# A hybrid decoder layer on one core: gate and up projections as seven products of half blocks

## The chip, the cores and the metric

The kernel runs on 1 core of one Trainium2 chip. The metric is the device time in microseconds (us) of one execution; lower is better. The five engines have queues of their own and run side by side: TensorE (PE in the profile), VectorE (DVE), ScalarE (ACT), GpSimd (POOL) and SyncE (SP), which issues nearly all DMAs here.

## The reference, cut to what matters

512 tokens of width 1024 in float32 pass through one layer: a norm and an input projection, two token mixers (a recurrence and a three-branch attention), an output projection with residual, and a SwiGLU feed-forward of width 2816. The change is in the last:

```python
D_MODEL = 1024; SEQ = 512; D_FF = 2816
h = rms_norm(x, ffn_norm_w[l])
x = x + (jax.nn.silu(h @ w_gate[l]) * (h @ w_up[l])) @ w_down[l]
```

## The kernel before, in words

All matrix operands are split into two float32r parts, `hi` (a rounded copy, made by ScalarE) and `lo` (the difference, made by a subtraction on VectorE or GpSimd), and a product of two such operands is three matmuls (`mm3`, L98). A weight tile of 512 KB comes through `load` (L111, SP's queue) into a `raw` tile, of which there are three, and `weights` (L130) makes its two parts: the cast on ScalarE (L146), the subtraction on VectorE or, in the input projection, GpSimd (L147). Activations of the feed-forward lie transposed in `ar`, as 8 chunks of 128 channels by two halves of 256 tokens, each in both parts.

The program's time falls in three stages. Up to about 180 us come the input projection and the recurrence, up to about 315 us the attention, a block of 128 tokens at a time (tiles 3, 2, 1, 0) with `out_proj` (L858) and `norm2` (L867) of a finished tile in between; `norm2` writes the second norm's transposes into `ar` (the subtraction is L885). Then SwiGLU: 11 groups of 256 hidden columns. `load_group` (L932) loads four raw tiles (gate and up, two halves of the channels); `gate_up` (L940) forms for each 128 columns the gate sums `fg` and the up sums `fu` over 8 chunks, 24 matmuls each, then the activation (L950 to L952) and the split of the result into `gh` and `gl` (L953, L107). The first two groups run by halves of the tokens, 256 columns at a time, so that tokens 256 to 511 go ahead while the attention of the others ends; the other nine take all 512. I call the gate and up work of 128 hidden columns a **unit**; there are 22.

```python
    for grp in range(SPLIT):
        load_group(grp)
        gate_up(grp, 256, 512, (4, 6), (5, 7))
    for grp in range(SPLIT):
        gate_up(grp, 0, 256, (4, 6), (5, 7))
    for grp in range(SPLIT, DF // 256):
        load_group(grp)
        gate_up(grp, 0, T, (4, 6, 0), (5, 7, 2))
```

The down projection (`fd`, L968 on) takes two halves of 512 output columns; each steps through the 22 blocks of `gh`, `gl` with four token tiles, and adds the residual from `x_sb` (L996). The order of instructions on each engine is set when the program is built, by a scheduler with a model of times; on the chip each engine takes its queue in that order.

Of the kernel before, what the change touches and what calls it, by code (L numbers as in the profile page):

```python
# [20 lines left out]
P = 128  # L21
T = 512
# [16 lines left out]
# rows of the packed parameter vectors  # L39
# [10 lines left out]
def hybrid_layer(ctx, tc, x, pos, pack, w_in, gate_a, gate_x, qnw, knw, ck1, ck2, cv1, cv2, w_out, fnw, w_gate, w_up, w_down, out):  # L50
# [5 lines left out]
    wst = ctx.enter_context(tc.tile_pool(name="wst", bufs=4))  # L56
# [11 lines left out]
    SLOTS = {"qk": 16, "yr": 8, "rt": 8, "y": 4, "tr": 6}  # L68
# [6 lines left out]
    def rot(s, banks):  # L75
        """the next of a set of banks that a kind of tile takes in turn"""
        rota[s] = rota.get(s, -1) + 1
        return bank(s, banks[rota[s] % len(banks)])

    def b2(s, dt=F32, tag="tr"):  # L80
        return big.tile([P, 512], dt, tag=tag, name=nm(s), bufs=SLOTS[tag])

# [12 lines left out]
    def mm(o, l, r, start, stop):  # L95
        PE.matmul(o, lhsT=l, rhs=r, start=start, stop=stop)  # L96

    def mm3(o, l, r, start, stop):  # L98
        mm(o, l[0], r[0], start, False)
        mm(o, l[0], r[1], False, False)  # L100
        mm(o, l[1], r[0], False, stop)
# [27 lines left out]

    def weights(src, a, b, lo_eng=None, row=None, halves=False):  # L130
        """rows of a weight matrix, scaled by the parameter column of each block of rows if there is one, as a pair of
        float32r parts whose sum is exact"""
        raw = wst.tile([P, 1024], F32, tag="raw", bufs=3, name=nm("raw"))
        rv = raw[:, : a * b].rearrange("p (a b) -> p a b", a=a)
        load(rv, src)
        hi = wst.tile([P, 1024], F32R, tag="whi", name=nm("whi"))
        lo = wst.tile([P, 1024], F32R, tag="wlo", name=nm("wlo"))
        n = a * b
        if row is not None:
# [8 lines left out]
        return [tuple(t[:, : a * b].rearrange("p (a b) -> p a b", a=a)[:, i] for t in (hi, lo)) for i in range(a)]  # L148

# [1 line left out]
    x_sb = per.tile([P, NT, D], F32, name="x_sb")  # L151
# [5 lines left out]
    def load_x(t):  # L157
        load(x_sb[:, t], x[t * P : (t + 1) * P])
# [83 lines left out]
    def proj_cm(c0, banks):  # L242
        """channel-major projection of 512 columns from c0: four banks [128 channels, 512 tokens]"""
# [27 lines left out]
    for t in range(NT):  # L271
        dg = b2("dg", tag="qk")[:, :P]
# [45 lines left out]
    # softplus(-lambda), accurately, for the four channel tiles  # L318
# [34 lines left out]
    # block-diagonal gate weights  # L353
    gwr = wst.tile([P, 8, P], F32, tag="raw", bufs=3, name="gwr")
# [5 lines left out]
    gwh = [b2("gwh", F32R, tag="qk") for _ in range(2)]  # L360
    gwl = [b2("gwl", F32R, tag="qk") for _ in range(2)]
# [14 lines left out]
    for m in range(4):  # L376
# [6 lines left out]
        h, l = b2("xch", F32R, tag="qk"), b2("xcl", F32R, tag="qk")  # L383
# [15 lines left out]
    def head_rstd(ss, nt):  # L399
        """ss [P, nt, heads]: sums of squares of raw projections -> factors that rms-normalise them, in place"""  # L400
# [14 lines left out]
    def rotate(raw, rs, t0, nt, rows=P):  # L415
        """raw [rows, heads, 64] times rs [rows, heads], then the rotation of nt groups of heads by table columns from t0"""
# [27 lines left out]
    # values of a block of keys, with a column of ones that yields the softmax's sums  # L444
# [6 lines left out]
    zs = []  # L451
    for m in range(4):
        z = b2("z", tag="qk")
# [17 lines left out]
    def recurrence_a():  # L471
        for m in range(4):
# [6 lines left out]
            # d = 1/(1+v): seed (1+a)/2 and one Newton step, kept negated  # L479
# [17 lines left out]
    def recurrence_b():  # L497
        for m in range(4):
            after(S.activation(vs_[m], vs_[m], AF.Sqrt), *tanhs)
        for m in range(4):  # L500
# [6 lines left out]
            h, l = b2("yrh", F32R, tag="yr"), b2("yrl", F32R, tag="yr")  # L507
# [43 lines left out]
    def key_part(src, t, br):  # L551
        """raw keys times the norm weight, and their sums of squares"""
# [6 lines left out]
    # rows that pick the negated maxima of a branch  # L559
# [6 lines left out]
    def keys(br, banks):  # L566
        """normalise, rotate, split, transpose -> [kh;kh] and [kl;sel]"""
        head_rstd(kss[br], NT)
        rotate(kraw[br].rearrange("p t h d -> p (t h) d"), kss[br].rearrange("p t h -> p (t h)"), 0, NT)
        for g in range(2):  # L570
# [5 lines left out]
            pair = []  # L576
            for z in (h, l):
# [19 lines left out]
    # compressed branch: operand tiles [(l mod 2, d), tokens]  # L597
# [41 lines left out]
    # second operand of the transposed scores: the queries' high parts, and rows for the negated maxima of each branch  # L639
# [12 lines left out]
    # compress MLPs  # L652
# [5 lines left out]
    for j in range(2):  # L658
# [5 lines left out]
        for kk in range(4):  # L664
            raw = wst.tile([P, 4, HID], F32, tag="raw", bufs=3, name=nm("raw"))
# [98 lines left out]
    def front(i, g, br):  # L764
        """row maxima of the scores of the four heads of a group, negated, into rows of the second operand: a list of steps"""
# [28 lines left out]
    def back(i, g, br):  # L794
        """transposed scores less the maxima, their exponentials and the products with the values: a list of steps"""
# [22 lines left out]
    def merge(i, g, br):  # L818
        """a branch's outputs, divided by the softmax's sums and gated"""
# [16 lines left out]
    def finish(i):  # L836
        """the norm's factor, and the outputs transposed and split"""
# [190 lines left out]
```

## Time and profile before

| | |
|---|---|
| time, median of 3 runs | 692.53 us (691.77 to 693.9) |
| profiled execution, span from first to last instruction | 691.3 us |
| time around the span, as median less span | 1.2 us |
| busy: PE, DVE, ACT, POOL | 657.2, 365.4, 240.6, 103.1 us |
| instructions in the span | 8803 |

The profile is of one execution of this kernel; the own time of that execution is not listed apart from the three runs, so its span and the median are set side by side. "Busy" is the time in which an engine had an instruction under way, waiting for a shared resource after it was issued included. Lines such as L96 or L107 are helpers that many steps share; which step a row belongs to is told by its tile names.

### The profile page before, as it was taken

What the parts mean: (1) busy time and instruction counts of PE and PEld (TensorE: products, weight loads), DVE (VectorE), ACT (ScalarE), POOL (GpSimd) and SP (SyncE); (2) the same over time, 40 slices, a digit from 0 to 9 for tenths busy, and PEclk for the clock granted to TensorE, in tenths of its full rate; (3) what the DMA queues carried; (4) which work ended last, traced back from release to release, by engine and by line L of the source; (5) the groups of instructions that cost most, each with busy time, mean ns of one, the idle gap of its engine ahead of it and who ended that gap; (6) DMA issues with size and microseconds to landing.
All of it is one profiled execution on the core that took longest, in us unless ns stands there. A gap on an engine that the chain in (4) does not pass through costs nothing.

```text
span 691.3 us, 8803 instructions
## 1 busy us (share of the span) xinstructions
PE 657.2 (95%) x3486; PEld 543.6 (79%) x3486; DVE 365.4 (53%) x713; ACT 240.6 (35%) x409; POOL 103.1 (15%) x95
## 2 busy tenths in 40 slices
PE   7998959598999999999999999999999999999998
PEld 6876848575777888879898888888888888888886
DVE  6779999956455758584723443334433442223211
ACT  5516753473433335353412232223322331112110
POOL 3426596223400101011000000000000000000000
PEclk9999989899999999999999999999999999999999
DMA  7343210324501201032402442244223423334301
GB/s 255 97 126 91 62 34 24 105 62 157 182 10 53 62 1 31 1 93 61 122 1 61 122 108 71 66 122 122 69 73 103 121 94 100 110 108 138 92 1 61
DMA packets 45185, 58.30 MB, mean 84 GB/s; under 512 B 3860, under 2 KB 31832, under 8 KB 45144
## 3 DMA queue, kind: packets, MB, share of 16 engines
q1 hardware_dynamic: 45064, 57.71, 27.6%
q8 instruction: 27, 0.44, 0.3%
q14 instruction: 14, 0.11, 0.0%
q10 hardware_dynamic: 80, 0.03, 0.0%
HBM read 55.64 MB, written 2.10 MB: 84 GB/s over the span
## 4 chain that ended last, share of the span: by engine, by line
PE 74%; DVE 15%; issue 4%; DMA 3%; ACT 2%; POOL 1%; SPq 0%; POOLq 0%; DVEq 0%; ACTq 0%
PE fd L96 18%; PE fu L96 17%; PE fg L96 17%; PE po L96 5%; PE por L96 3%; PE sT L96 3%; PE pw L96 2%; PE s L96 2%; PE ph L96 2%; PE ptm L96 2%; DMA raw<-in_w_in_dram 1%; DVE xc L382 1%; DVE tg L484 1%; DMA raw<-in_cv_dram 1%; DVE tg L503 1%
## 5 line engine op out<-in xcount | busy, mean ns | idle before, releaser
L146 ACT CAST whi<-raw 128x1024 fp32r<-128x1024 f32 (+2 forms) x85 | 86.7, 1024 | 157.6 <-PE fd L96 75.4
L147 DVE TENSOR_TENSOR wlo<-raw,whi 128x1024 fp32r<-128x1024 f32 (+1 forms) x63 | 76.1, 1208 | 115.9 <-ACT whi L146 115.9
L96 PE MATMUL fu<-ar,whi 128*128 128x512 f32 (+1 forms) x352 | 101.9, 374 | 0.0
L96 PE MATMUL fg<-ar,whi 128*128 128x512 f32 x288 | 90.5, 395 | 0.0
L96 PEld LDWEIGHTS fu<-ar,whi 128*128 128x128 f32 x352 | 63.8, 188 | 13.1
L96 PE MATMUL fd<-wlo,gh 128*128 128x512 f32 (+1 forms) x189 | 69.3, 367 | 0.0
L96 PE MATMUL fd<-whi,gh 128*128 128x512 f32 (+1 forms) x189 | 69.2, 366 | 0.0
L96 PE MATMUL fd<-whi,gl 128*128 128x512 f32 (+1 forms) x189 | 68.9, 366 | 0.0
L96 PE MATMUL fu<-ar,wlo 128*128 128x512 f32 (+1 forms) x176 | 65.8, 374 | 0.0
L96 PEld LDWEIGHTS fg<-ar,whi 128*128 128x128 f32 x288 | 54.1, 188 | 13.0
L96 PE MATMUL ptm<-whi,ar 128*128 128x512 f32 (+1 forms) x192 | 56.1, 374 | 7.7 <-DVE qraw L526 7.7
L147 POOL TENSOR_TENSOR wlo<-raw,whi 128x1024 fp32r<-128x1024 f32 (+1 forms) x22 | 51.0, 2327 | 46.0 <-ACT whi L146 25.3
L96 PE MATMUL fg<-ar,wlo 128*128 128x512 f32 x144 | 57.0, 396 | 0.0
L96 PEld LDWEIGHTS ptm<-whi,ar 128*128 128x128 f32 x192 | 36.3, 198 | 13.6 <-DVE qraw L526 8.1
L96 PE MATMUL pcm<-ar,whi 128*128 128x512 f32 (+1 forms) x160 | 42.1, 354 | 1.4 <-DVE ar L226 1.0
L952 DVE SCALAR_TENSOR_TENSOR ft<-ft,fu 128x512 f32<-128x512 f32 (+1 forms) x26 | 15.7, 606 | 48.9 <-PE fu L96 48.9
L96 PE MATMUL po<-va,pe 128*128 128x65 f32 x320 | 41.1, 272 | 0.0
L96 PEld LDWEIGHTS po<-va,pe 128*128 128x128 f32 x320 | 39.7, 192 | 1.7 <-ACT pe L809 0.8
L96 PEld LDWEIGHTS fd<-whi,gh 128*128 128x128 f32 x189 | 35.6, 189 | 6.1
L96 PEld LDWEIGHTS fd<-wlo,gh 128*128 128x128 f32 x189 | 35.6, 189 | 5.9
L96 PEld LDWEIGHTS fd<-whi,gl 128*128 128x128 f32 x189 | 35.6, 188 | 5.9
L96 PEld LDWEIGHTS fu<-ar,wlo 128*128 128x128 f32 x176 | 33.1, 188 | 6.6
(315 smaller groups left out, 1149.4 us busy)
## 6 DMA issues: line engine op xcount, KB each, us to landing
raw<-in_w_gate_dram SPq DMA_DIRECT2D x22, 512.0 KB, 3.8
raw<-in_w_up_dram SPq DMA_DIRECT2D x22, 512.0 KB, 3.8
raw<-in_w_down_dram SPq DMA_DIRECT2D x22, 512.0 KB, 3.8
raw<-in_w_in_dram SPq DMA_DIRECT2D x16, 512.0 KB, 4.5
raw<-in_w_out_dram SPq DMA_DIRECT2D x8, 512.0 KB, 4.3
x_sb<-in_x_dram SPq DMA_DIRECT2D x4, 512.0 KB, 8.6
raw<-in_ck_dram SPq DMA_DIRECT2D x4, 512.0 KB, 3.9
raw<-in_cv_dram SPq DMA_DIRECT2D x4, 512.0 KB, 4.2
```

Source lines behind the costliest of these rows:

```text
L96: PE.matmul(o, lhsT=l, rhs=r, start=start, stop=stop)
L146: S.copy(hi[:, c], raw[:, c])
L147: (lo_eng or V).tensor_tensor(out=lo[:, c], in0=raw[:, c], in1=f(hi[:, c]), op=ALU.subtract)
L382: V.scalar_tensor_tensor(out=c[:, s:], in0=xr[:, : T - s], scalar=col(R_CW + 4 * k + m), in1=c[:, s:], op0=ALU.mult, op1=ALU.add)
L484: V.scalar_tensor_tensor(out=e, in0=v, scalar=1.0, in1=u, op0=ALU.subtract, op1=ALU.mult)
L503: V.tensor_tensor_scan(out=bx, data0=a, data1=bx, initial=0.0, op0=ALU.mult, op1=ALU.add)
L952: V.scalar_tensor_tensor(out=tt, in0=tt, scalar=0.5, in1=pu[:, :nn], op0=ALU.mult, op1=ALU.mult)
```

## The change

The gate rows and the up rows of a unit are stacked, and channels and tokens are halved: A11, A12 are the gate weights of channels 0 to 511 and 512 to 1023, A21, A22 the up weights; B11, B21 are the two channel halves of tokens 256 to 511, B12, B22 those of tokens 0 to 255. The 2 by 2 block product, eight half products, is formed as seven, by Strassen's identity in Winograd's form: A11 B11, A12 B21, S1 T1, S2 T2, S3 T3, S4 B22 and A22 T4 (the sign of T4 turned), with sums of weight blocks S1 to S4 and of activations T1 to T4, and sums of products afterwards.

- Weights: a unit loads `r1` (gate) and `r2` (up), 128 columns each, 512 KB each, into `raw` tiles, of which there are still three. GpSimd forms the four sums (`sums`), and ScalarE and VectorE split `r1`, `sb` (S2, S4), `sa` (S1, S3) and half of `r2` (`split`). Their tiles come from one set of 12 (`w`) in place of two sets of 4.
- Products: 7 times 12 matmuls of 256 columns, in three accumulators. ScalarE copies five intermediate values out of PSUM, GpSimd adds three of them (L1091 to L1093), VectorE the last two (L1028, L1029), then the activation follows (L1032 to L1034).
- `norm2`: the last two tiles (tokens 0 to 255) form T1 to T4 and transpose five tiles each in place of two.
- The gate weights of the first three units are loaded twice, and their products A11 B11 and A12 B21 go ahead of the rest, in place of the two groups by halves.
- The gated values stay unsplit until the end of the stage; `gh` and `gl` are then made in space that the operands leave. The residual is stored to DRAM by `out_proj` and loaded back in the down projection, which adds four stores and four loads of 512 KB.

The core of the diff (helpers and renamings left out):

```diff
-    wst = ctx.enter_context(tc.tile_pool(name="wst", bufs=4))
+    wst = ctx.enter_context(tc.tile_pool(name="wst", bufs=12))
...
+    def raw_tile(s):
+        return wst.tile([P, 1024], F32, tag="raw", name=nm(s), bufs=3)
+    def w_tile(s, dt=F32R):
+        return wst.tile([P, 1024], dt, tag="w", name=nm(s))
...
             V.scalar_tensor_tensor(out=xs, in0=pw, scalar=ra, in1=xs, op0=ALU.mult, op1=ALU.add)
+        load(x2_dram[i * P : (i + 1) * P], x_sb[i])
...
+        V.tensor_tensor(out=t3, in0=xn[1], in1=xn[0], op=ALU.subtract)
+        V.tensor_tensor(out=xn[0], in0=xn[0], in1=xo[0], op=ALU.subtract)
+        V.tensor_tensor(out=t2, in0=xn[1], in1=xn[0], op=ALU.subtract)
+        V.tensor_tensor(out=xo[1], in0=xo[1], in1=t2, op=ALU.subtract)
+        for src, n in ((t2, "T2"), (xn[0], "T1"), (t3, "T3"), (xo[1], "T4"), (xn[1], "22")):
+            put(src, n)
...
+    def split(t, c=slice(0, 1024), mk=w_tile):
+        hi, lo = mk("h"), mk("l")
+        i1 = S.copy(hi[:, :n], t[:, c])
+        i2 = V.tensor_tensor(out=lo[:, :n], in0=t[:, c], in1=f(hi[:, :n]), op=ALU.subtract)
...
+    def sums(u, r1):
+        r2, sa, sb = raw_tile("r2"), x_tile("sa"), x_tile("sb")
+        w_cols(w_up, u, r2)
+        G.tensor_tensor(out=sa[:, :512], in0=a21, in1=a22, op=ALU.add)
+        G.tensor_tensor(out=sb[:, :512], in0=sa[:, :512], in1=a11, op=ALU.subtract)
+        G.tensor_tensor(out=sb[:, 512:], in0=a12, in1=sb[:, :512], op=ALU.subtract)
+        G.tensor_tensor(out=sa[:, 512:], in0=a11, in1=a21, op=ALU.subtract)
...
+    for u in range(NU + 1):
+        if u < NU:
+            r1 = gate_weights(u)
+            ss = sums(u, r1)
+            if u >= EARLY:
+                set_gate(u, r1)
+                p_a(u, 1)
+            set_sums(u, *ss)
...
+            product(acc_b[u], u, "S2", "T2", True)
+            S.copy(e, acc_b[u])
+            if u >= EARLY:
+                p_a(u, 2)
+        if u > 0:
+            product(acc_b[u - 1], u - 1, "22", "T4", False)
+            product(acc_c[u - 1], u - 1, "S4", "22", False)
+            finish_unit(u - 1)
+        if u < NU:
+            product(acc_c[u], u, "S1", "T1", True)
+            S.copy(s5, acc_c[u])
+            product(acc_b[u], u, "S3", "T3", False)
+            S.copy(fv, acc_b[u])
+            G.tensor_tensor(out=e, in0=e, in1=s1, op=ALU.add)
+            G.tensor_tensor(out=fv, in0=fv, in1=s1, op=ALU.add)
+            G.tensor_tensor(out=s5, in0=s5, in1=fv, op=ALU.add)
```

What the scheduler makes of it, at three places of the SwiGLU stage. First GpSimd's queue. Before, these rows are its last in the program: the end of the attention and the two factors of `norm2`, with no work for SwiGLU.

```order
L834 TENSOR_TENSOR y_2930<-y_2930,oc_sb_2873 128x256 x2
L196 TENSOR_TENSOR ra_3034<-ms_3035,nhalf 128x1
L196 TENSOR_TENSOR r_609_3082<-ms_3083,nhalf 128x1
L196 TENSOR_TENSOR r_617_3109<-ms_3110,nhalf 128x1
L1024 UNCONDITIONAL_BRANCH
```

Now GpSimd has seven instructions for each unit. Around the 9th unit (`r_840`, `r_841` are its `r1`, `r2`; L996 to L999 are the four sums, L1091 to L1093 the adds of earlier products):

```order
L996 TENSOR_TENSOR sa_4706<-r_841_4705 128x512
L999 TENSOR_TENSOR sa_4706<-r_840_4703,r_841_4705 128x512
L1093 TENSOR_TENSOR xa_4482<-xa_4482,xb_4483 128x256
L997 TENSOR_TENSOR sb_4707<-sa_4706,r_840_4703 128x512
L1091 TENSOR_TENSOR xb_4613<-xb_4613,xa_4612 128x256
L998 TENSOR_TENSOR sb_4707<-r_840_4703,sb_4707 128x512
```

Two of the small adds now stand between the sums, and the last sum of a unit is the last reader of its `r1`.

Second, VectorE's queue in the same stage. Before, one group, that is two units (four subtractions for the weights, then activation and split of each unit):

```order
L147 TENSOR_TENSOR wlo_4080<-raw_4077,whi_4079 128x1024
L147 TENSOR_TENSOR wlo_4086<-raw_4083,whi_4085 128x1024
L951 SCALAR_TENSOR_TENSOR ft_4071<-ft_4071,fg_4021 128x512
L147 TENSOR_TENSOR wlo_4092<-raw_4089,whi_4091 128x1024
L952 SCALAR_TENSOR_TENSOR ft_4071<-ft_4071,fu_4022 128x512
L147 TENSOR_TENSOR wlo_4098<-raw_4095,whi_4097 128x1024
L107 TENSOR_TENSOR gl_3964<-ft_4071,gh_3963 128x512
L951 SCALAR_TENSOR_TENSOR ft_4155<-ft_4155,fg_4105 128x512
```

Now, about one unit (L975 are the subtractions of `split`; `fb`, `fc` lie in PSUM, all other tiles in SBUF):

```order
L975 TENSOR_TENSOR l_4454<-r_802_4443,h_4453 128x1024
L1033 SCALAR_TENSOR_TENSOR xb_4223<-ft_4407,xb_4223 128x512
L1028 TENSOR_TENSOR xa_4222<-fb_4225,xa_4222 128x256
L1034 SCALAR_TENSOR_TENSOR g_4182<-xb_4223,xa_4222 128x512
L975 TENSOR_TENSOR l_4471<-sb_4447,h_4470 128x1024
L975 TENSOR_TENSOR l_4475<-sa_4446,h_4474 128x1024
L975 TENSOR_TENSOR l_4479<-r_803_4445,h_4478 128x512
```

One unit now has three and a half subtractions of 1024 columns where it had two, and the activation's instructions read SBUF alone.

Third, SP's queue of loads. Before, in the same stage:

```order
L112 DMA raw_3937<-in_w_gate_dram 128x4x256
L112 DMA raw_3943<-in_w_gate_dram 128x4x256
L112 DMA raw_3949<-in_w_up_dram 128x4x256
L112 DMA raw_3955<-in_w_up_dram 128x4x256
L112 DMA raw_4077<-in_w_gate_dram 128x4x256
```

Now:

```order
L118 DMA r_764_4183<-in_w_gate_dram 128x8x128
L118 DMA r_765_4185<-in_w_up_dram 128x8x128
L118 DMA r_783_4313<-in_w_gate_dram 128x8x128
L118 DMA r_784_4315<-in_w_up_dram 128x8x128
L118 DMA r_802_4443<-in_w_gate_dram 128x8x128
```

The bytes of a unit are the same; a contiguous run is 128 columns (512 B) in place of 256, and with three `raw` tiles a unit's `r2` takes the place of the unit before's `r1`.

## Rows read from the trace of the kernel before

**Rows 1.** The page: span, and busy time of each engine (share of span, instructions).

```profile
span 691.3 us, 8803 instructions
...
PE 657.2 (95%) x3486; PEld 543.6 (79%) x3486; DVE 365.4 (53%) x713; ACT 240.6 (35%) x409; POOL 103.1 (15%) x95
```

**Rows 2.** Chain that ended last, in order of time: start us, us, what.

```profile
359.83 2.72 PE fg L96 x24
...
561.26 5.60 PE fu L96 x24
566.86 121.08 PE fd L96 x594
```

**Rows 3.** Stretches: us, busy us of each engine (count), granted clock, DMA share, GB/s.

```profile
325.00:344.00 19.00, 18.05 (x130) 16.43 (x129) 12.85 (x21) 8.60 (x16) 0.76 (x1) 1.00 0.39 111
...
365.00:460.00 95.00, 95.00 (x410) 76.60 (x409) 38.38 (x44) 27.25 (x34) 0.00 (x0) 1.00 0.35 99
567.00:691.30 124.30, 120.92 (x594) 102.14 (x592) 29.98 (x30) 20.25 (x20) 0.00 (x0) 1.00 0.28 89
```

**Rows 4.** Timeline of DVE, last write of `norm2` into `ar`: start us, us, what.

```profile
344.60 0.69 DVE L885 TENSOR_TENSOR ar<-h2p,ar 128x512 fp32r<-128x512 f32 x1 [1.04 <-ACT ar L884]
```

**Rows 5.** Groups by form, late stages, DVE and ACT: count | busy us, mean ns.

```profile
L147 DVE TENSOR_TENSOR wlo<-raw,whi 128x1024 fp32r<-128x1024 f32 x60 | 73.5, 1225 | 115.1 <-ACT whi L146 115.1
L952 DVE SCALAR_TENSOR_TENSOR ft<-ft,fu 128x512 f32<-128x512 f32 x18 | 12.4, 689 | 44.1 <-PE fu L96 44.1
...
L107 DVE TENSOR_TENSOR wxl<-raw,wxh 128x512 fp32r<-128x512 f32 x10 | 6.6, 682 | 0.5 <-ACT wxh L125 0.3 <-PE sT L96 0.2
...
L146 ACT CAST whi<-raw 128x1024 fp32r<-128x1024 f32 x60 | 63.3, 1055 | 141.1 <-PE fd L96 75.4 <-PE fg L96 27.0 <-PE fu L96 16.8
```

**Rows 6.** Timeline of POOL, three instructions on two SBUF operands.

```profile
36.25 2.40 POOL L147 TENSOR_TENSOR wlo<-raw,whi 128x1024 fp32r<-128x1024 f32 x1 [2.56 <-ACT whi L146]
...
100.81 1.30 POOL L502 TENSOR_TENSOR tg<-tg,v 128x512 f32<-128x512 f32 x1
...
318.22 0.74 POOL L834 TENSOR_TENSOR y<-y,oc_sb 128x256 f32<-128x256 f32 x1 [4.58 <-DVE y L833]
```

**Rows 7.** Timelines of POOL and DVE at four places where both have work.

```profile
105.98 2.40 POOL L147 TENSOR_TENSOR wlo<-raw,whi 128x1024 fp32r<-128x1024 f32 x1
106.01 2.91 DVE L505 TENSOR_TENSOR z<-z,tg 128x512 f32<-128x512 f32 x1
...
112.66 1.51 POOL L513 TENSOR_TENSOR v<-v,v 128x512 f32<-128x512 f32 x1 [4.29 <-ACT v L506]
113.00 1.72 DVE L509 SCALAR_TENSOR_TENSOR yrl<-z,rwn,yrh 128x512 fp32r<-128x512 f32 x1
...
52.27 1.40 DVE L382 SCALAR_TENSOR_TENSOR xc<-xr,par,xc 128x509 f32<-128x509 f32 x2
53.25 3.32 POOL L147 TENSOR_TENSOR wlo<-raw,whi 128x1024 fp32r<-128x1024 f32 x1 [10.15 <-PE pcm L96]
53.59 0.69 DVE L107 TENSOR_TENSOR xcl<-xc,xch 128x512 fp32r<-128x512 f32 x1
...
96.34 2.81 POOL L147 TENSOR_TENSOR wlo<-raw,whi 128x1024 fp32r<-128x1024 f32 x1
96.85 0.68 DVE L526 TENSOR_TENSOR qraw<-ptm,qw 128x512 f32<-128x512 f32 x1
```

**Rows 8.** DMA issues: out<-in, queue, count, KB each, median us to landing.

```profile
raw<-in_w_gate_dram SPq DMA_DIRECT2D x22, 512.0 KB, 3.8
```

**Rows 9.** Stretches as in rows 3, around three pauses of PE.

```profile
62.10:65.40 3.30, 0.01 (x1) 0.01 (x1) 3.09 (x15) 1.24 (x3) 0.00 (x0) 1.00 0.58 159
89.90:97.50 7.60, 0.02 (x1) 0.00 (x0) 7.60 (x8) 5.35 (x9) 7.24 (x5) 0.81 0.00 0
97.50:104.50 7.00, 6.92 (x23) 5.56 (x24) 7.00 (x9) 4.46 (x7) 7.00 (x5) 0.72 0.16 42
163.80:166.20 2.40, 0.40 (x3) 0.28 (x3) 2.37 (x5) 0.68 (x1) 1.59 (x1) 1.00 0.84 280
166.20:169.60 3.40, 3.40 (x9) 1.48 (x7) 2.14 (x4) 0.00 (x0) 1.96 (x3) 0.50 0.35 117
```

More of the change, by code (lines that the diff above doesn't have):

```diff
@@ L93, in after, with mm, mm3 @@
         return ins
[L95 to L101, printed above, removed]
+    def mm(o, l, r, start, stop, **kw):
+        PE.matmul(o, lhsT=l, rhs=r, start=start, stop=stop, **kw)
+    def mm3(o, l, r, start, stop, **kw):
+        mm(o, l[0], r[0], start, False, **kw)
+        mm(o, l[0], r[1], False, False, **kw)
+        mm(o, l[1], r[0], False, stop, **kw)
     def tp(o, i, n=P):
@@ L157, in load_x @@
     def load_x(t):
[L158 removed]
+        load(x_sb[t], x[t * P : (t + 1) * P])
     load_x(0)
@@ L451, in hybrid_layer @@
     zs = []
+    zp = [b4("z") for _ in range(2)]
     for m in range(4):
-        z = b2("z", tag="qk")
+        z = zp[m // 2][m % 2]
         V.tensor_tensor(out=z, in0=gr_ps[m], in1=rbc, op=ALU.mult)
@@ new lines, in hybrid_layer, with gate_weights @@
+    chain = {}
+    def split(t, c=slice(0, 1024), mk=w_tile):
+        hi, lo = mk("h"), mk("l")
+        n = c.stop - c.start
+        i1 = S.copy(hi[:, :n], t[:, c])
+        i2 = V.tensor_tensor(out=lo[:, :n], in0=t[:, c], in1=f(hi[:, :n]), op=ALU.subtract)
+        for k, i in (("S", i1), ("V", i2)):
+            if k in chain:
+                after(i, chain[k])
+            chain[k] = i
+        return [(hi[:, c * P : (c + 1) * P], lo[:, c * P : (c + 1) * P]) for c in range(n // P)]
+    def gate_weights(u):
+        r1 = raw_tile("r1")
+        w_cols(w_gate, u, r1)
+        return r1
@@ new lines, in set_sums, with product, half @@
+    def set_sums(u, r2, sa, sb):
+        o = split(sb)
+        A[u]["S2"], A[u]["S4"] = o[:4], o[4:]
+        o = split(sa)
+        A[u]["S1"], A[u]["S3"] = o[:4], o[4:]
+        A[u]["22"] = split(r2, slice(512, 1024))
+    def product(o, u, a, b, start):
+        for c in range(4):
+            mm3(o, A[u][a][c], tuple(z[:, c] for z in B[b]), start and c == 0, c == 3, skip_group_check=not start)
+    def half(s, n):
+        return bank(s, n)[:, :256]
+    acc_a, acc_b, acc_c = {}, {}, {}
@@ new lines, in p_a, with finish_unit @@
+    def p_a(u, n):
+        if n == 1:
+            acc_a[u] = half("fa", 4 + u % 4)
+            product(acc_a[u], u, "11", "11", True)
+        else:
+            product(acc_a[u], u, "12", "21", False)
+    def finish_unit(u):
+        gate, up, s1, e, ft = hold[u]
+        V.tensor_tensor(out=up[:, 256:], in0=acc_b[u], in1=s1, op=ALU.add)
+        V.tensor_tensor(out=gate[:, :256], in0=acc_c[u], in1=e, op=ALU.add)
+        if ft is None:
+            ft = cst.tile([P, 544], F32, tag="misc", name=nm("ft"), bufs=3)[:, :512]
+        S.activation(ft, gate, AF.Tanh, scale=0.5)
+        V.scalar_tensor_tensor(out=gate, in0=ft, scalar=1.0, in1=gate, op0=ALU.add, op1=ALU.mult)
+        V.scalar_tensor_tensor(out=gs[u], in0=gate, scalar=0.5, in1=up, op0=ALU.mult, op1=ALU.mult)
@@ new lines, in hybrid_layer, with g_tile @@
+    gtags = [t for t in ("gx", "y", "rt") for _ in range(SLOTS[t])]
+    def g_tile(u):
+        if u < 4:
+            if u % 2 == 0:
+                gs.extend(b4("g"))
+        else:
+            gs.append(b2("g", tag=gtags.pop()))
+    ahead = {}
+    for u in range(EARLY):
+        mk = w_tile if u < 2 else (lambda s: big.tile([P, 1024], F32R, tag="qk", name=nm(s), bufs=8))
+        set_gate(u, gate_weights(u), mk)
+        p_a(u, 1)
+        xe = cst.tile([P, 544], F32, tag="misc", name=nm("xe"), bufs=3)[:, :512]
+        S.copy(xe[:, :256], acc_a[u])
+        p_a(u, 2)
+        S.copy(xe[:, 256:], acc_a[u])
+        ahead[u] = xe
@@ L966, in hybrid_layer @@
     NK = DF // P
     TAIL = 4
+    gl_tags = ["tr"] * 2 + ["qk"] * 4 + ["rt"] * 8 + ["y"] * 4 + ["gx"] * 4
+    gh_at = [z.rearrange("p c q -> p (c q)")[:, o : o + 512] for n in ("11", "T2", "T1", "21", "T3", "T4") for z in B[n] for o in (0, 512)]
+    gh = []
+    for k in range(NK):
+        h = gh_at[k]
+        S.copy(h, gs[k])
+        if gl_tags[k] == "qk":
+            if k % 2 == 0:
+                pair = b4("gl", F32R)
+            l = pair[k % 2]
+        else:
+            l = b2("gl", F32R, tag=gl_tags[k])
+        lo_of(l, gs[k], h)
+        gh.append((h, l))
```

215 lines of the change are left out of this document (115 added, 100 removed).

## The prediction

> **What bounds the kernel now.** I read the page first: PE is busy for 657.2 of 691.3 us, POOL for 103.1 [rows 1]. An average over stages doesn't price a change in one of them, so next I read the chain of waits in order of time, from its end backwards: from 345 us on it holds nothing but matmuls. A set of 24 takes 5.60 us at 512 columns and 2.72 us at 256, so 233 and 113 ns per matmul; the down projection is 121.08 us from 566.86 [rows 2]. The stretches agree: PE has 95.0 of 95 us, DVE 38, ACT 27 and POOL nothing, at a granted clock of 1.00, the upper level of 2.4 GHz [rows 3]. The attention's end is covered too (18.05 of 19 us). So PE bounds SwiGLU now, and fewer columns would be worth their full time if nothing else took over. POOL's empty column is where the change puts work, so the last views are POOL's and DVE's timelines where both have work [rows 7].
>
> **The yardstick.** `norm2`'s last write ends at 344.60 + 0.69 = 345.3 us [rows 4]. From there the rest of gate and up takes 221.6 us, down 121.1, the end of the span 3.4 more (691.3 - 687.9), and the median is 1.2 above the span. That is 345.3 + 221.6 + 121.1 + 3.4 + 1.2 = 692.6. I replace the second and third terms.
>
> **PE's part.** A unit had 48 matmuls of 512 columns, 11.2 us; it has 84 of 256, 84 x 0.1133 = 9.52 us. Over 22 units that saves 37 us on PE, if PE stays the bound.
>
> **POOL's part.** A unit gets four sums of 512 columns and three adds of 256, both operands in SBUF. Such instructions took 1.30 and 0.74 us [rows 6], so 4 x 1.30 + 3 x 0.74 = 7.42 us. Alone this fits under 9.52.
>
> **DVE's part.** A unit has three subtractions of 1024 columns (1.225), one of 512 (0.68) and two activation steps of 512 (0.69, that of a form with one PSUM operand) [rows 5]: 3 x 1.225 + 0.68 + 2 x 0.69 = 5.74 us, all on SBUF operands alone. The two adds L1028, L1029 read PSUM and come on top. Alone this fits too.
>
> **The two together do not.** The first pair [rows 7]: POOL starts a subtraction at 105.98 and ends at 108.38; DVE's instruction, issued at 106.01 and worth 0.68, shows 2.91 us and ends at 108.92, half a microsecond after POOL. In the second, POOL ends at 114.17 and DVE's 113.00 instruction at 114.72. In the third it is the other way round: POOL's instruction, 2.40 us alone [rows 6], shows 3.32, and the excess of 0.92 is the time until DVE's `xcl`, a subtraction of exactly the `lo` form, is done. In the fourth DVE's instruction has a PSUM operand and is not held: 0.68. So on SBUF operands these two engines take turns, whole instruction by whole instruction. A unit then needs 7.42 + 5.74 = 13.16 us of turns. Records overlap by 0.08 us ([rows 7], a DVE instruction starts at 53.59, the one before ends at 52.27 + 1.40 = 53.67), 13 of them by 1.0, which leaves 12.1 us if no turn is ever empty. One is: after a unit's last sum, DVE's next subtraction waits for ACT's cast of that sum, 1.06 us [rows 5], while POOL's next sum waits for a load. I take 12.1 + 0.9 = **13.0 us per unit**, and keep 12.1 (no empty turn) and 14.2 (full records and a full cast) as ends.
>
> No row shows a subtraction of the `lo` form, with its float32r result, held behind a running POOL instruction; the rows have only POOL held behind it. The Trainium skill has a rule for this (SBUF — State Buffer, section "Who interferes with whom"): a DVE instruction with two SBUF inputs contends with a GpSimd instruction that reads SBUF, and whoever issues first has the shared ports for the whole instruction. By that rule the direction without a row holds too and the period stays at 13.0; if the `lo` form could pass under POOL, turns would be 7.42 + 1.38 = 8.8 us and the first rival below would rule.
>
> **SP's part.** `r2` of a unit lands where the unit before's `r1` was, so it is issued after that unit's last sum; the first sum of the unit then waits for it. A 512 KB load lands in 3.8 us [rows 8]. Runs get half as long: 0.35 [rows 3] x 16 engines x 95 us over 9.4 MB is 58 ns per 1 KB run, 0.28 x 16 x 124.3 over 11.1 MB is 103 ns per 2 KB run, so on a straight line 35 ns per 512 B run, and 1024 of them on 16 engines 2.3 us in place of 1.9: 4.2 us to landing. This ring, load, four sums and the two small adds that stand between them, is 4.2 + 5.2 + 1.5 = 10.9 us, under 13.0, so I give the loads nothing (bound: at double the landing, 7.6, the ring is 14.3). Four stores, four loads of the residual and three repeated gate loads of 512 KB pass through the same queue, 0.35 busy now; nothing, up to 2 us each where one sits ahead of a waited load.
>
> **Around the stage.** The last two tiles of `norm2` gain four subtractions on DVE and three sets of transposes each, some 4 x 0.69 + 3 x 0.69 = 4.8 us for the last one, in the open; against that PE has 3 x 24 x 0.113 = 8.2 us of early products to place among the attention's end in place of 4 x 48 x 0.113 = 21.8. I let these cancel, between -6 and +6, and keep 345.3 as the start. The tiles shared anew in the first stages (12 in place of 8, of which four are lent out) I take as nothing, between -5 and +5. The first three units' `r1` was split ahead: 3 x 1.23 = 3.7 us off. At the end, 40 matmuls of the down projection stand in PE's queue ahead of the last products, in time that PE has left: 40 x 0.229 = 9.2 us off down. Casting and splitting 22 blocks for `gh`, `gl` lies beside 112 us of matmuls, 22 x 0.69 us on DVE [rows 5]: nothing.
>
> **The sum.** 345.3 + 22 P - 3.7 + (121.1 - 9.2) + 3.4 + 1.2 = 458.1 + 22 P. With P = 13.0 this is **744 us**, 51 more than now. The ends of P give 724 and 770. Faster and slower meet at P = 10.66.
>
> **Rivals.**
> - *Faster or equal, no turns between sums and splits* (the `lo` form passes under POOL, or POOL's forms here don't collide). The ring rules, P = 10.5 to 10.9, so 689 to 698; were the ring short too, PE would: 345.3 + 22 x 9.52 - 8.2 + 121.1 + 3.4 + 1.2 = 672. For it: only three held forms [rows 7], none the sums' own. Against: POOL waited for the `lo` form there. It decides at 10.66 us per unit. Chance 0.08, of it 0.05 below 690.5.
> - *Slower still, PE's clock falls.* PE now waits 3.5 us per unit. A pause of 7.6 us was followed by a granted clock of 0.72 over 7 us, a stretch with 0.40 of 2.4 us busy by 0.50, the lower level of 1.2 GHz, for 3.4 us, and a pause of 3.3 us passed at 1.00 [rows 9]. At the lower level for a third of the time a unit's matmuls take 3.2 us more; half of it on the path makes P = 14.6 and 779 us, all of it 814. Chance 0.11.
> - *The change isn't what it says.* 22 x 84 matmuls of 256 columns stand in the queue, seven eighths of the columns before; under 0.01.
>
> The forecast has 0.80. The measurement can tell about 0.3%, 2 us: faster 0.05, same 0.03, slower 0.92. The range takes in the ends of P, the 6 and 5 us around the stage and half of the clock's case: 716 to 776.
>
> **What would show it.** Right: a unit every 13 us in the stage; PE about 72% busy there; DVE's L975 and L1033, L1034 and POOL's L996 to L999 well over 1.23, 0.69 and 1.30 us on average; PE's waits ending at ACT's cast of `sb`. Wrong: L975 at 1.23 beside a busy POOL and a period under 11 us; a granted clock under 1.00 through the stage; or `fd` starting later than the units' end.

## The result, and the profile after

| | before | after |
|---|---|---|
| time, median of 4 runs | 692.35 us (691.77 to 693.9) | 732.49 us (732.12 to 736.98) |
| profiled execution, span | 691.3 us | 730.7 us |
| one unit in the steady stage | 11.2 us | 12.70 us |

The changed kernel is slower: its time is 1.0587 times that of the kernel before, with a 95% interval of 1.0555 to 1.0619. The forecast was 744 us in a range of 716 to 776.

The page of the changed kernel, span and busy time of each engine (share of the span, instructions):

```profile
span 730.7 us, 10547 instructions
...
PE 655.2 (90%) x4110; PEld 573.4 (78%) x4110; DVE 483.9 (66%) x797; ACT 307.1 (42%) x555; POOL 329.3 (45%) x249
```

Against [rows 1] the busy time of PE is almost the same, although it has an eighth fewer columns in gate and up. DVE has 118 us more and POOL 226 us more. The stretch of the steady stage shows who fell back (columns as in [rows 3]):

```profile
420.00:560.00 140.00, 120.21 (x934) 118.24 (x933) 97.31 (x90) 61.74 (x109) 115.47 (x78) 0.93 0.29 83
```

PE stands idle 20 of 140 us, where [rows 3] had none, and neither DVE nor POOL is busy all the time. No single engine is the bound. The groups by form between 360 and 600 us (count | busy us, mean ns of one | idle us before them, and what ended it) show what the busy time is made of:

```profile
L975 DVE TENSOR_TENSOR l<-r,h 128x1024 fp32r<-128x1024 f32 x19 | 38.0, 1999 | 1.3 <-ACT h L974 1.3
...
L997 POOL TENSOR_TENSOR sb<-sa,r 128x512 f32<-128x512 f32 x19 | 33.4, 1757 | 0.0
L975 DVE TENSOR_TENSOR l<-sa,h 128x1024 fp32r<-128x1024 f32 x19 | 31.7, 1669 | 0.0
L996 POOL TENSOR_TENSOR sa<-r 128x512 f32<-128x512 f32 x18 | 31.4, 1746 | 8.0 <-DMA r<-in_w_up_dram 8.0
...
L1093 POOL TENSOR_TENSOR xa<-xa,xb 128x256 f32<-128x256 f32 x20 | 30.7, 1535 | 0.8
...
L999 POOL TENSOR_TENSOR sa<-r,r 128x512 f32<-128x512 f32 x18 | 27.8, 1546 | 0.0
...
L975 DVE TENSOR_TENSOR l<-sb,h 128x1024 fp32r<-128x1024 f32 x19 | 23.3, 1225 | 43.3 <-ACT h L974 43.3
...
L1033 DVE SCALAR_TENSOR_TENSOR xb<-ft,xb 128x512 f32<-128x512 f32 x17 | 21.5, 1264 | 13.5 <-ACT ft L1032 13.5
...
L1034 DVE SCALAR_TENSOR_TENSOR g<-xb,xa 128x512 f32<-128x512 f32 x17 | 12.1, 714 | 0.9
...
L1028 DVE TENSOR_TENSOR xa<-fb,xa 128x256 f32<-128x256 f32 x17 | 7.1, 418 | 9.4 <-PE fb L102 9.4
```

The same form, L975 with 1024 columns, takes 1225 ns on `sb` and 1999 ns on `r`. POOL's sums take 1.55 to 1.76 us where one was worth 1.30 [rows 6], and its adds of 256 columns 1.54 in place of 0.74. The form with an operand in PSUM (L1028) takes 0.42. One unit in order of time shows how these means come about. First POOL's timeline (start us, us, what, and in brackets the idle time before it with what ended it):

```profile
452.34 1.74 POOL L998 TENSOR_TENSOR sb<-r,sb 128x512 f32<-128x512 f32 x1
...
460.36 1.32 POOL L999 TENSOR_TENSOR sa<-r,r 128x512 f32<-128x512 f32 x1
461.62 2.29 POOL L997 TENSOR_TENSOR sb<-sa,r 128x512 f32<-128x512 f32 x1
463.87 1.16 POOL L1091 TENSOR_TENSOR xb<-xb,xa 128x256 f32<-128x256 f32 x1
465.00 1.25 POOL L998 TENSOR_TENSOR sb<-r,sb 128x512 f32<-128x512 f32 x1
468.90 0.88 POOL L1092 TENSOR_TENSOR xb<-xb,xa 128x256 f32<-128x256 f32 x1 [2.65 <-ACT xb L1090]
...
477.74 1.74 POOL L998 TENSOR_TENSOR sb<-r,sb 128x512 f32<-128x512 f32 x1
```

And DVE's beside it:

```profile
460.65 2.11 DVE L975 TENSOR_TENSOR l<-r,h 128x1024 fp32r<-128x1024 f32 x1
462.68 1.78 DVE L1033 SCALAR_TENSOR_TENSOR xb<-ft,xb 128x512 f32<-128x512 f32 x1
467.36 1.23 DVE L975 TENSOR_TENSOR l<-sb,h 128x1024 fp32r<-128x1024 f32 x1 [2.91 <-ACT h L974]
```

Read them together. DVE's L975, issued at 460.65, waits until POOL's L999 is done at 461.68 and ends at 462.76, 1.1 later. POOL's L997, issued at 461.62, waits for that one and ends at 463.91. DVE's L1033, issued at 462.68, waits for L997 and ends at 464.46. POOL's L1091 waits for L1033 and ends at 465.03. Then DVE has nothing at hand, and L998 takes its own 1.25. Each record is its own time plus the other engine's instruction ahead of it, less an overlap of some 0.15 us.

After L998 (465.00 + 1.25 = 466.25) neither engine has an instruction on SBUF until 467.36: 1.11 us, while ScalarE casts `sb`. DVE waits for that cast, and POOL, whose next is the add L1092, for a copy out of PSUM (L1090) that ScalarE starts at 468.45, after the cast. From 427 to 554 us, ten units, the two timelines laid over each other show ten such gaps, each of 1.10 or 1.11 us, and no other. Two units, from L998 at 452.34 to L998 at 477.74, take 25.40 us, so one takes 12.70.

### The profile page after: what moved, and what is told of

It is laid out like the page before. It is cut to its first block, busy times and chain, and to the rows that moved or that the text cites. A ratio compares the mean times of both kernels' runs of the same rounds, so it can differ in the third digit from the quotient of the medians.

```text
span 730.7 us, 10547 instructions
## 1 busy us (share of the span) xinstructions
PE 655.2 (90%) x4110; PEld 573.4 (78%) x4110; DVE 483.9 (66%) x797; ACT 307.1 (42%) x555; POOL 329.3 (45%) x249
## 4 chain that ended last, share of the span: by engine, by line
PE 45%; POOL 23%; DVE 12%; DMA 8%; issue 7%; ACT 4%; POOLq 0%; ACTq 0%; DVEq 0%
PE fd L102 17%; DMA r<-in_w_up_dram 6%; PE po L102 5%; POOL sb L997 5%; POOL sb L998 4%; POOL sa L999 4%; PE sT L102 3%; PE por L102 3%; PE pw L102 3%; POOL xb L1091 3%; POOL xa L1093 3%; PE pcm L102 2%; PE s L102 2%; POOL sa L996 2%; PE ph L102 2%
## 5 line engine op out<-in xcount | busy, mean ns | idle before, releaser
L102 PE MATMUL fb<-T,h 128*128 128x256 f32 x352 | 71.7, 300 | 36.3 <-ACT h L974 34.2
L102 PEld LDWEIGHTS fb<-T,h 128*128 128x128 f32 x352 | 57.9, 202 | 40.1 <-ACT h L974 37.6
L143 ACT CAST whi<-raw 128x1024 fp32r<-128x1024 f32 (+2 forms) x47 | 46.5, 1001 | 75.2 <-PE fd L102 55.9
L975 DVE TENSOR_TENSOR l<-r,h 128x1024 fp32r<-128x1024 f32 (+1 forms) x44 | 72.5, 1650 | 1.9 <-ACT h L974 1.9
L102 PE MATMUL ptm<-whi,ar 128*128 128x512 f32 (+1 forms) x192 | 58.7, 388 | 12.1 <-DVE qraw L531 9.1
L144 POOL TENSOR_TENSOR wlo<-raw,whi 128x1024 fp32r<-128x1024 f32 (+1 forms) x22 | 52.1, 2378 | 30.7 <-ACT whi L143 22.5
L102 PE MATMUL fa<-ar,h 128*128 128x256 f32 x352 | 65.4, 284 | 0.0
L975 DVE TENSOR_TENSOR l<-sb,h 128x1024 fp32r<-128x1024 f32 x22 | 27.1, 1230 | 50.4 <-ACT h L974 50.4
L144 DVE TENSOR_TENSOR wlo<-raw,whi 128x1024 fp32r<-128x1024 f32 (+1 forms) x25 | 29.6, 1186 | 45.5 <-ACT whi L143 45.5
L102 PEld LDWEIGHTS fa<-ar,h 128*128 128x128 f32 x352 | 55.4, 194 | 0.1
L102 PE MATMUL fb<-T,l 128*128 128x256 f32 x176 | 51.6, 293 | 0.8 <-DVE l L975 0.8
L102 PE MATMUL fa<-ar,l 128*128 128x256 f32 x176 | 49.8, 283 | 0.4 <-DVE l L975 0.4
L1092 POOL TENSOR_TENSOR xb<-xb,xa 128x256 f32<-128x256 f32 x19 | 28.2, 1486 | 42.5 <-ACT xb L1090 42.5
L996 POOL TENSOR_TENSOR sa<-r 128x512 f32<-128x512 f32 x22 | 36.7, 1667 | 23.3 <-DMA r<-in_w_up_dram 21.8
L974 ACT CAST h<-r 128x1024 fp32r<-128x1024 f32 (+1 forms) x44 | 36.8, 841 | 8.7 <-PE fc L102 4.6
```

The source lines that it names most:

```text
L102: PE.matmul(o, lhsT=l, rhs=r, start=start, stop=stop, **kw)
L143: S.copy(hi[:, c], raw[:, c])
L144: (lo_eng or V).tensor_tensor(out=lo[:, c], in0=raw[:, c], in1=f(hi[:, c]), op=ALU.subtract)
L974: i1 = S.copy(hi[:, :n], t[:, c])
L975: i2 = V.tensor_tensor(out=lo[:, :n], in0=t[:, c], in1=f(hi[:, :n]), op=ALU.subtract)
L996: G.tensor_tensor(out=sa[:, :512], in0=a21, in1=a22, op=ALU.add)
```

## The experiments

The **turns theory** is the prediction's: DVE's instructions with all operands in SBUF and POOL's on SBUF exclude each other, and the sum of their durations, with a gap of 1.11 us, is the unit. The rival that the trace still allows is the **load ring**: the chain that ended last in the changed kernel also holds the load of `r2`, which waits for the unit before's last sum (start us, us, what):

```profile
466.28 3.74 DMA r<-in_w_up_dram
```

Each run below was timed beside the kernel before; the unit's period is read from the timeline of `sb`'s last sum, over two to ten units of the steady stage. In e3 and e8 it is that of most units: two of twelve take 10.5 to 10.7 us, with a wait of VectorE for a late load of `r2`, and the mean is 9.97. A change of the time is not 22 times that of the unit. From the end of the 4th unit's last sum to that of the 22nd's the changed kernel takes 228.0 us, e3 180.2 and e9 212.5. So e3 gains 47.8 and e9 15.5 us in these 18 units, where the whole times differ by 52.1 and 13.6.

| run | edit | unit, us | time, us | ratio to before (95%) |
|---|---|---|---|---|
| after | | 12.70 | 732.5 | 1.0587 (1.0555 to 1.0619) |
| e4 | fourth `raw` tile | 12.40 | 730.0 | 1.054 (1.0496 to 1.0584) |
| e1 | small adds on DVE, from PSUM | 11.15 | 707.4 | 1.0211 (1.0171 to 1.0251) |
| e2 | sums on DVE | 10.04 | 683.7 | 0.9874 (0.9844 to 0.9905) |
| e3 | sums and adds on DVE | 9.83 | 680.4 | 0.9823 (0.9792 to 0.9854) |
| e5 | after, DVE fillers on SBUF | 13.1 | 746.7 | 1.0771 (1.074 to 1.0802) |
| e6 | after, DVE fillers on PSUM | 12.78 | 732.4 | 1.0565 (1.0545 to 1.0585) |
| e7 | e3, POOL fillers that read | 13.70 | 762.4 | 1.1006 (1.0976 to 1.1036) |
| e8 | e3, POOL fillers that write only | 9.84 | 679.9 | 0.9809 (0.9787 to 0.9831) |
| e9 | `sb` split in halves | 11.8 | 718.9 | 1.0378 (1.0347 to 1.041) |

**e4, is it the load ring?**

```diff
-        return wst.tile([P, 1024], F32, tag="raw", name=nm(s), bufs=3)
+        return wst.tile([P, 1024], F32, tag="raw", name=nm(s), bufs=4)
...
-        xa = small([P, 8, 16], "rpa", bufs=2)[:rows, :nh]
-        xb = small([P, 8, 16], "rpb", bufs=2)[:rows, :nh]
+        xa = small([P, 8, 16], "rpa", bufs=1)[:rows, :nh]
+        xb = small([P, 8, 16], "rpb", bufs=1)[:rows, :nh]
```

> The changed kernel with a fourth `raw` tile (the space comes from two small scratch tiles of the attention, held once in place of twice). A unit's `r2` then no longer waits for the unit before's last sum to be done. Turns theory: the 3.9 us between a unit's last sum and the next unit's first are no loss, since VectorE's three subtractions use them; the sum of the turns is the same, so the unit keeps its 12.7 us and the time stays at 725 to 734. Load-ring theory (the load of `r2` that waits for the last sum sets the pace): the 3.9 us go from the ring, the next bound is PE's 9.5 us or GpSimd's own 7.4, and the time falls to 665 to 690.

730.0 us: the load ring isn't the bound. The loads came earlier, the sums began earlier, and now collided with DVE's subtractions where before they had followed them. Two rows of the groups by form, 400 to 560 us:

```profile
L975 DVE TENSOR_TENSOR l<-sa,h 128x1024 fp32r<-128x1024 f32 x13 | 30.1, 2314 | 0.0
L999 POOL TENSOR_TENSOR sa<-r,r 128x512 f32<-128x512 f32 x13 | 29.6, 2274 | 0.0
```

The subtraction went from 1669 to 2314 ns and the sum from 1546 to 2274: the time that the load no longer took came back as waiting for the other engine. The unit did fall by 0.30 us. The queues have another order in this build, and the two timelines show 0.73 us per unit without a turn in place of 1.11. What is left, 12.40 - 0.73 = 11.67 us, is close to the 12.69 - 1.11 = 11.58 of the changed kernel.

**e1, e2 and e3, work taken from POOL.** e1 moves the adds, e2 the sums, e3 both:

```diff
-            S.copy(e, acc_b[u])
+            V.tensor_tensor(out=e, in0=acc_b[u], in1=s1, op=ALU.add)
...
-            S.copy(s5, acc_c[u])
...
-            S.copy(fv, acc_b[u])
-            G.tensor_tensor(out=e, in0=e, in1=s1, op=ALU.add)
-            G.tensor_tensor(out=fv, in0=fv, in1=s1, op=ALU.add)
-            G.tensor_tensor(out=s5, in0=s5, in1=fv, op=ALU.add)
+            V.tensor_tensor(out=fv, in0=acc_b[u], in1=s1, op=ALU.add)
+            V.tensor_tensor(out=s5, in0=acc_c[u], in1=fv, op=ALU.add)
```

```diff
-        G.tensor_tensor(out=sa[:, :512], in0=a21, in1=a22, op=ALU.add)
...
+        V.tensor_tensor(out=sa[:, :512], in0=a21, in1=a22, op=ALU.add)
...
```

> The changed kernel with the three small adds of a unit taken from GpSimd to VectorE, where they read the product straight out of PSUM (three ScalarE copies go too). Turns theory: 3 x 0.74 less 3 x 0.08 = 2.0 us of turns go per unit, and VectorE's 0.41 us with a PSUM operand take no turn: about 10.7 us per unit and 688, with 680 to 705 allowed for a new order of the queues. Load-ring theory: only the two adds that stand between the sums leave the ring, 2 x 1.2 us as they are seen now, so 10.3 us per unit, 680. The mean of one sum on GpSimd should stay well above 1.30 us by the turns theory.

> The changed kernel with the four sums on VectorE in place of GpSimd; GpSimd keeps the three small adds. Turns theory: a sum of 512 columns takes 0.69 there in place of 1.30, so turns per unit are 4 x 0.69 + 5.74 + 3 x 0.74 = 10.7 less overlaps of 0.08, about 10.0 us, and the time 670 to 690, although VectorE alone now has 10.7 us of work and GpSimd nearly none. A theory in which GpSimd is only slow, without turns, gives the same sign but lets L1091 to L1093 show 0.74 us again; by turns they stay above it.

> Both at once: sums and small adds on VectorE, GpSimd without work in the stage. VectorE alone has 4 x 0.69 + 5.74 + 5 x 0.41 = 10.55 us of records, 14 of them with 0.06 to 0.08 of overlap, so about 9.5 us per unit, level with PE's 9.5. Turns theory: 9.6 to 10.2 us per unit, 665 to 685, faster than the kernel before, with every VectorE form back at its own duration (1.23, 0.69, 0.68). If something other than the shared use of SBUF ports held the unit at 12.7 us (load ring, lower clock of PE), the time would stay above 700.

e2 and e3 came where the turns theory put them, and both beat the kernel before, by 1.3 and 1.8% with intervals clear of 1. e1 fell as far as 707 us, 2 us outside what was allowed: its unit took 11.15 us in place of 10.7. Over two units, 22.3 us, the two timelines show 2.3 us without a turn under way, 1.15 us per unit: the 1.11 us once, and six gaps of 0.1 to 0.26 where DVE runs its new PSUM adds while POOL waits for a tile or a load. A turn must be at hand to be taken; the sum of the turns alone is a lower end.

e2 shows turns from the other side. Its rows between 400 and 560 us, where POOL has only the small adds left:

```profile
L1092 POOL TENSOR_TENSOR xb<-xb,xa 128x256 f32<-128x256 f32 x16 | 21.1, 1316 | 100.1 <-ACT xb L1090 100.1
...
L975 DVE TENSOR_TENSOR l<-r,h 128x512 fp32r<-128x512 f32 x15 | 17.8, 1186 | 0.0
```

An add of 0.74 us still shows 1.32, and the subtraction beside it 1.19 in place of 0.68. With POOL empty, in e3, that same form is back at its own time (400 to 560 us):

```profile
L975 DVE TENSOR_TENSOR l<-r,h 128x512 fp32r<-128x512 f32 x15 | 10.3, 685 | 0.0
```

And the stretch of e3's stage shows what is left as the bound:

```profile
420.00:560.00 140.00, 138.72 (x1152) 136.95 (x1152) 132.51 (x212) 73.45 (x117) 0.00 (x0) 1.00 0.41 124
```

PE is busy for 99% of it at a granted clock of 1.00, with DVE close behind at 95%; no run parts the two. This is the version to use of those here: 680.4 us, 12 us under the kernel before.

**e5 and e6, dummy work on DVE.** Both add to the changed kernel, ahead of the activation, work that only the activation's own write passes over:

```diff
+        for z in range(2):
+            V.tensor_tensor(out=ft, in0=fbc[:, :512], in1=fbc[:, 512:], op=ALU.add)
```

```diff
+        for z in (acc_b[u], acc_c[u], acc_b[u], acc_c[u]):
+            V.tensor_tensor(out=ft[:, :256], in0=z, in1=fbc[:, :256], op=ALU.add)
```

> The changed kernel with two more VectorE additions of 512 columns per unit, both operands in SBUF, whose result only the activation's later write passes over. VectorE stands idle 4.7 of a unit's 12.7 us now, and 2 x 0.68 us would fit there. Turns theory: they take turns from GpSimd, 2 x (0.68 - 0.08) = 1.2 us per unit, 26 us in all, so about 758; down to 745 where one fills a turn that is empty now. Without turns (GpSimd's own queue or the load ring as the bound) they lie in idle time: 728 to 738.

> The counterpart: four more VectorE additions of 256 columns per unit with one operand in PSUM, 4 x 0.41 = 1.64 us of records, more of VectorE's time than in the run with the two SBUF additions. Turns theory: an operand in PSUM takes no turn, so they lie in idle time and the time stays at 728 to 740, far below the run with the two SBUF additions. A theory in which VectorE's whole load counts beside GpSimd's (any instruction, not the SBUF port) expects 4 x 0.33 x 22 = 29 us more, 760.

The two on SBUF cost 14 us, the four on PSUM nothing, though DVE had idle time for either (3.9 us per unit in the stretch of the steady stage, not the 4.7 of the expectation). The two on SBUF filled the gap of 1.11 us in every second unit (four are left in 100 us), so of their 1.2 us per unit 0.55 fell into empty turns, and the unit grew by 0.4. Over 22 units that is 9 us. Most of the rest lies outside the steady stage: near its start two units take 29.4 us between the ends of their last sums (368.34 to 397.69), where the changed kernel's take 25.8. The row of each, 400 to 560 us, first e5:

```profile
L1033 DVE TENSOR_TENSOR ft<-fbc 128x512 f32<-128x512 f32 x27 | 31.0, 1151 | 0.0
```

and e6:

```profile
L1033 DVE TENSOR_TENSOR ft<-fc,fbc 128x256 f32<-128x256 f32 x26 | 11.0, 423 | 0.8
```

With both operands in SBUF the mean is 1.15 in place of 0.68; with one in PSUM it is 0.42, like L1028.

**e7 and e8, dummy work on POOL.** Here nobody waits for the added work at all. It goes into e3, where POOL is empty, and writes to the half of a split tile that no one reads:

```diff
+        if n == 512:
+            for z in range(4):
+                G.tensor_tensor(out=lo[:, 512:], in0=fbc[:, :512], in1=fbc[:, 512:], op=ALU.add)
```

```diff
+        if n == 512:
+            for z in range(10):
+                G.memset(f(lo[:, 512:]), 0)
```

> The version with sums and adds on VectorE (680 us), and four additions of 512 columns per unit on GpSimd that read SBUF and whose result nobody reads (it goes to the unused half of a split tile). Turns theory: VectorE's SBUF forms, 8.5 us of records or 7.6 without overlaps, and 4 x 1.25 us take turns, so at least 12.6 us per unit: 735 to 770, with VectorE's SBUF forms far above their own durations and its PSUM forms at 0.41. Without turns nobody waits for these four, and the time stays at 677 to 684.

> As the run before, but with ten fills of 512 columns per unit on GpSimd in place of the four additions: GpSimd is as busy (a fill of 1024 columns took 0.95 us in the trace, so 10 x 0.5 = 5 us) but reads nothing. If only GpSimd's reads take turns with VectorE's second operand, the time stays at 677 to 685. If any GpSimd instruction takes the turn, 7.6 + 10 x 0.45 = 12.1 us per unit, 725 to 760.

The reading fillers cost 82 us, the writing ones nothing. One unit of e7, POOL's timeline:

```profile
457.02 7.46 POOL L982 TENSOR_TENSOR l<-fbc 128x512 fp32r<-128x512 f32 x4 [6.20 <-PE fb L102]
```

and DVE's beside it:

```profile
457.32 1.55 DVE L1037 SCALAR_TENSOR_TENSOR g<-xb,xa 128x512 f32<-128x512 f32 x1
458.79 2.32 DVE L975 TENSOR_TENSOR l<-sb,h 128x1024 fp32r<-128x1024 f32 x1
461.03 0.41 DVE L1093 TENSOR_TENSOR xa<-fc,xb 128x256 f32<-128x256 f32 x1
461.37 1.97 DVE L975 TENSOR_TENSOR l<-sa,h 128x1024 fp32r<-128x1024 f32 x1
463.26 1.77 DVE L999 TENSOR_TENSOR sa<-r 128x512 f32<-128x512 f32 x1
```

Over their own times (0.68, 1.22, 1.22 and 0.69 in e3) DVE's four SBUF forms lose 0.87 + 1.10 + 0.75 + 1.08 = 3.80 us; the unit is 13.70 - 9.83 = 3.87 us longer. That accounts for nearly all of it. The PSUM form between them took 0.41 with POOL busy beside it. In e8 POOL is as busy (79 us of 160), and DVE's form stays at its own time:

```profile
L982 POOL MEMSET l<- 128x512 f32 x150 | 79.1, 527 | 70.1 <-PE fb L102 62.3
...
L975 DVE TENSOR_TENSOR l<-sb,h 128x1024 fp32r<-128x1024 f32 x15 | 18.3, 1218 | 0.0
```

The Trainium skill (SBUF — State Buffer, section "Who interferes with whom") says that a DVE instruction with two SBUF inputs contends with GpSimd instructions that read SBUF, and not with those that only write it. The pair e7 and e8 agrees with both halves, 762.4 against 679.9 us.

**e9, the empty turn.**

```diff
-        i1 = S.copy(hi[:, :n], t[:, c])
-        i2 = V.tensor_tensor(out=lo[:, :n], in0=t[:, c], in1=f(hi[:, :n]), op=ALU.subtract)
+        for z in (slice(0, 512), slice(512, 1024)) if parts else (slice(0, n),):
+            i1 = S.copy(hi[:, z], t[:, c][:, z])
+            i2 = V.tensor_tensor(out=lo[:, z], in0=t[:, c][:, z], in1=f(hi[:, z]), op=ALU.subtract)
...
-        o = split(sb)
+        o = split(sb, parts=True)
```

> The changed kernel with the split of `sb` in two halves, each cast and subtracted on its own, so that the first half (S2) can go while GpSimd still forms the second (S4). In the trace of the changed kernel no engine has a turn for 1.11 us in each unit, from the end of a unit's last sum to the end of ScalarE's cast of `sb`; with halves VectorE has work then. Turns theory: 0.5 to 1.11 us less per unit, one more hand-over of 0.05 us added, so 10 to 23 us less, 709 to 722. If the empty turn is not what is lost there (the load ring, or PE's wait for the whole of `sb`), the time stays at 729 to 736.

718.9 us, 13.6 less, and over 100 us of the stage a single gap of 0.83 us is left, where POOL waits for a load of `r2`. POOL's last sum of a unit (L999 here) on its timeline:

```profile
458.07 2.25 POOL L999 TENSOR_TENSOR sb<-r,sb 128x512 f32<-128x512 f32 x1
...
469.97 2.14 POOL L999 TENSOR_TENSOR sb<-r,sb 128x512 f32<-128x512 f32 x1
```

and DVE's first half of `sb` beside the first of them:

```profile
459.44 1.43 DVE L976 TENSOR_TENSOR l<-sb,h 128x512 fp32r<-128x512 f32 x1
```

DVE now has the first half at hand before the last sum has ended, and goes on as soon as it has, at 460.3. The unit went from 12.70 to 11.8 us, so 0.9 of the 1.11 us came back.

## Why the prediction was right

The mechanism, its place and the size held. Term by term, from the changed kernel's trace: the last write of `norm2`, the rest of the down projection in the chain that ended last, and the last sums of the first two units, beside the attention:

```profile
344.46 0.68 DVE L897 TENSOR_TENSOR ar<-h2pb,ar 128x512 fp32r<-128x512 f32 x1
```

```profile
615.22 112.22 PE fd L102 x554
```

```profile
296.50 1.27 POOL L998 TENSOR_TENSOR sb<-r,sb 128x512 f32<-128x512 f32 x1
...
340.94 1.27 POOL L998 TENSOR_TENSOR sb<-r,sb 128x512 f32<-128x512 f32 x1
```

- **The start**, 345.3: `norm2`'s last write ended at 345.1. The two effects that were left to cancel did so together; neither was measured on its own.
- **P**, 13.0: 12.70. Own times were taken as 13.16 us of turns, less 0.08 for each of 13 hand-overs, 12.1. Measured are 12.69 - 1.11 = 11.58 over ten units, so 0.12 per hand-over. The empty turn was taken as 0.9 and is 1.11, ScalarE's whole cast with its signals. The two misses are of opposite sign and cancel in part, by luck. What POOL waits for in the empty turn was read wrong: ScalarE's copy for the add L1092, which stands ahead of the next sum in POOL's queue, and not a load. No other turn was empty, so neither the units' loads, which landed in 3.8 us and not in 4.2, nor the added stores and loads in SP's queue cost anything beyond it.
- **22 P - 3.7**, 282.3: from 345.1 to 615.2 are 270.1. Of the 12.2 us, 22 x 0.30 = 6.6 come from P. The other 5.6 lie outside the steady units, and are the one term that was missed. The sums of the first two units were done before 345.1, the first at 296.50 while the attention still ran, so the stage didn't begin with whole units of turns. How much of the 5.6 this is, beside what the stage's end takes, was not taken apart. They fall within the 6 and 5 us that the range left around the stage.
- **The down projection**, 111.9: 112.2, with 40 of its matmuls ahead of the last products, as counted.
- **The end**, 3.4 + 1.2: 3.3 (730.7 - 727.4), and 1.8 from span to median.

The sum is 345.1 + 270.1 + 112.2 + 3.3 + 1.8 = 732.5.

The direction that no row had shown, a subtraction of the `lo` form held behind a running POOL instruction, is in the first row of the groups by form: 1999 ns. Of the rivals, the one without turns (689 to 698) would have needed L975 at 1.23 beside a busy POOL. It is excluded by e7 against e8. Its second half, PE as the bound at 672 us, is what e3 comes near when the turns are gone: 680.4, with 9.83 us per unit in place of 9.52.

The rival on PE's clock came half true without a price. It was named as a sign of being wrong if it lasted through the stage, and it came in spells: after a wait of PE the granted clock fell to 0.50, its lower level of 1.2 GHz, for some microseconds (columns as in [rows 3]):

```profile
463.50:467.40 3.90, 0.87 (x9) 0.68 (x7) 0.99 (x2) 1.11 (x2) 2.75 (x3) 0.87 0.01 2
467.40:473.00 5.60, 5.60 (x26) 5.60 (x27) 5.60 (x6) 3.26 (x6) 3.73 (x3) 0.50 0.31 92
```

The unit didn't grow from it. Two pairs of units, one without a spell and the one that this spell falls in:

```profile
415.49:440.86 25.37, 20.16 (x168) 19.77 (x168) 17.74 (x16) 11.30 (x20) 20.80 (x14) 1.00 0.29 84
466.25:491.65 25.40, 22.59 (x168) 22.39 (x168) 17.44 (x16) 11.51 (x20) 20.86 (x15) 0.87 0.28 83
```

PE's matmuls take 2.4 us more in the second, in time that PE had to spare, and the pair takes 25.40 us in place of 25.37. The clock is a part of why PE shows 86% busy in the stage where 72% had been announced. It isn't all: at 1.00 PE shows 20.16 of 25.37 us, 79%, or 120 ns per matmul in place of 113, and no run shows why.

Of the means that were announced as well over their own durations one is not: L1034 takes 714 ns, where 690 was taken as its own. L975 as a whole is at 1.63 us ((38.0 + 31.7 + 23.3) / 57), but on `sb` it keeps 1225 ns. That one always starts into the empty turn, with POOL waiting. And PE's waits end where they were said to, at ScalarE's cast of `sb` (who waited for whom between 360 and 600 us: us in total, times, longest):

```profile
PE fb L102 <- ACT h L974: 34.2, 17, 3.6
```

## What to carry to other kernels

Before putting element-wise work on an idle GpSimd, add up its own durations and those of VectorE's instructions whose operands all lie in SBUF, stage by stage: where both engines have such work, that sum, with the moments when neither has an instruction at hand, is a bound of its own, and the busy shares don't show it (45% and 66% here). A sum that costs VectorE 0.69 us cost 1.30 on GpSimd, so under this bound moving it to the idle engine made things worse, and moving the four of a unit back gained 49 us. An operand read straight from PSUM takes VectorE's instruction out of the sum (e1, e6). Splitting a step, so that a piece is at hand when the other engine ends, doesn't shorten the sum; it takes out moments when neither has an instruction at hand (e9).

## What was not expected of the hardware

- GpSimd's fills did not disturb VectorE at all: ten of 0.53 us per unit left the unit at 9.84 us (9.83 without them), where four reading additions made it 13.70.
- Hand-overs between the two engines are cheap: 13 instructions per unit that kept passing the turn to and fro took 0.12 us less each than their own durations add up to, with no cost of the change seen.
- The scalar-tensor-tensor form (L1033) is held like the plain subtraction: 1264 ns in place of 691 ns.
- PE's matmuls of 256 columns took about 9.83 x 0.99 / 84 = 116 ns each in e3 at a granted clock of 1.00, where the kernel before had shown 113 [rows 2]. Why was not tried.
